# Expert matrix products of a small half tile in four column quarters, and the next slot table formed beside the transposes of the current one

## The chip, the cores and the metric

The kernel runs on one core of a Trainium2 chip. The metric is the device time of one launch in microseconds (us), as the median of three runs. A trace of one further execution shows what each engine did: PE is the matrix engine (PEld its weight loads), DVE the vector engine, ACT the scalar engine, POOL the GpSimd engine, SP the queue that issues the loads.

## What is computed

Two transformer layers over 256 tokens of width 1024. The change touches only the last part, the expert layer of layer 2:

```python
def moe_swiglu(h, router, w_gu, w_d):                 # h: 256 tokens x 1024
    logits = jnp.einsum("bld,de->ble", h, router, preferred_element_type=jnp.float32)
    top_v, top_i = lax.top_k(logits, TOP_K)            # 2 of 8 experts for each token
    top_w = jax.nn.softmax(top_v, axis=-1)
    gates = jnp.sum(jax.nn.one_hot(top_i, N_EXPERTS, dtype=jnp.float32) * top_w[..., None], axis=-2)
    y = gates[..., 0:1] * swiglu(h, w_gu[0], w_d[0])
    for e in range(1, N_EXPERTS):
        y = y + gates[..., e:e + 1] * swiglu(h, w_gu[e], w_d[e])
    return y
def swiglu(h, w_gu, w_d):
    g, u = jnp.split(h @ w_gu, 2, axis=-1)             # 1024 -> 2 x 3584
    return (jax.nn.silu(g) * u) @ w_d                  # 3584 -> 1024
```

All data are float32. The router decides at run time how many tokens an expert has. For the inputs of the reference, worked out by running it, experts 0 to 7 have 68, 69, 55, 38, 145, 46, 29 and 62 tokens.

## The kernel before

**Loads.** The expert weights come from HBM in loads of 128 x 2048 float32 (1024 KB) through a ring of seven buffers (`raw...`, `mraw`); class `Stream` issues a load (line 79) as soon as PE has used up the buffer that it goes into.

**Steps.** Each expert is seven steps; a step is four loads for the gate and up products (`products`, one load each) and two for the down product (`down`). The 56 steps are sorted so that about three experts interleave: in the middle they run as trios such as (4,3), (5,1), (3,6), expert and step. Iteration n of the main loop does the products of step n, with the transposes of step n-1 (`turned`) after the second load, then the gate function of step n (`gated`), then `down` of step n-1.

**Modes.** `modes` chooses at run time by branches. An expert with over 64 tokens has a *full* tile of 128 token slots: its weights are split on ACT and DVE into a high and a low part (lines 102 and 106) and each load is 12 matmuls of 128 columns in the fast float32r format (L1188 to L1190, down L1243 to L1245). Up to 64 remaining tokens make a *half* tile, multiplied in plain float32 without a split (L1196, down L1251): each load is four matmuls with a stationary operand of 64 columns, and the trace shows each as two MATMUL records. Gate and up products go to output partitions 0 to 63 and 64 to 127 of one PSUM tile `PO`, so two matmuls sit side by side in PE's columns. Experts 0 and 1 are full, 2, 3, 5, 6 and 7 half, and 4 is both (128 + 17 tokens).

**Items.** Other work is put into numbered turns, three to a step (3n and 3n+1 ahead of `down`, 3n+2 behind it), at most one item to a turn. For each next expert e there are seven: `prep_p(e)` forms the slot table `P` on DVE (one-hot of token against slot, L1031 and L1033), four `prep_x` gather the tokens by matmuls with `P` (L1041), `prep_g` scales `P` by the gates on POOL (L1054), and `prep_t` transposes it on PE (L1061). `P` has one buffer. Four `scatter` items add an expert's result back (L1109, L1120).

The order on each engine is that of the code: an engine waits in front of an instruction and everything behind it waits as well.

Of the kernel before, what the change touches and what calls it, by code (L numbers as in the profile page):

```python
# [136 lines left out]
def backbone_kernel(ctx, tc, xT, small, const, moe_const, gmw, gmb, modk, modd, wa, wg2, wg4, wo, fgu, fd, mgu, mdn, fing, out):  # L137
# [769 lines left out]
    rank = mo.tile([128, 2, 8], F32, name="rank")  # L907
    rank_h = mo.tile([128, 2, 8], F32, name="rank_h")
    cnt = mo.tile([128, 25], I32, name="cnt")
    none = mo.tile([128, 8], BF16, name="none")  # L910
# [106 lines left out]
    def place(turn, fs):  # L1017

        for f in fs:
            while turn in items:  # L1020
                turn += 1
            items[turn] = f
            turn += 1

    TOGETHER = NS - 3

    def prep_p(e, bank=None):

        P = mp.tile([128, 2, NX], F32, name="P")
        for i in range(2):  # L1030
            nc.vector.tensor_scalar(P[:, i, 0:128], slots, rank[:, i, e:e + 1], None, op0=OP.is_equal)  # L1031
            side = P[:, i, 128:256].rearrange("p (a b) -> p a b", a=2)
            nc.vector.tensor_scalar(side, slots[:, None, 0:64].to_broadcast([128, 2, 64]), rank_h[:, i, e:e + 1], None, op0=OP.is_equal)  # L1033
        X[e] = dict(P=P, x=mp.tile([128, KD, NX], F32R, name="Xe", bufs=LANES), xo=mp.tile([128, KD, 64], F32, name="Xo", bufs=LANES))

    def prep_x(e, d, bank):

        P = X[e]["P"]
        for n in range(2):
            for i in range(2):  # L1040
                mm(bank[:, n * NX:n * NX + SLOTS], tm[:, i, (d + n) * 128:(d + n + 1) * 128], P[:, i, 0:SLOTS], start=i == 0, stop=i == 1)  # L1041
        xe, xo = X[e]["x"][:, d:d + 2], X[e]["xo"][:, d:d + 2]
        v = bank.rearrange("p (n c) -> p n c", n=2)

        def split():
            nc.scalar.copy(xe[:, :, 0:128], v[:, :, 0:128])
            nc.scalar.copy(xo, v[:, :, 128:SLOTS])
            nc.vector.tensor_tensor(xe[:, :, 128:256], v[:, :, 0:128], xe[:, :, 0:128].bitcast(F32), op=OP.subtract)
        post.append(split)
# [6 lines left out]
    def prep_t(e, bank):  # L1056

        P = X[e]["P"]
        for s in range(2):
            for i in range(2):  # L1060
                nc.tensor.transpose(bank[:, s * NX + i * 128:s * NX + (i + 1) * 128], P[:, i, s * 128:(s + 1) * 128], ident)  # L1061
        X[e]["T"] = pt = mp.tile([128, 2, NX], F32, name="Pt", bufs=LANES + 1)
        post.append(lambda: nc.scalar.copy(pt.rearrange("p a b -> p (a b)"), bank))

    def row_halves(a):
# [58 lines left out]

    def modes(e, full, half, bank=None):

        with tc.If(full_[e] > 0) as c:
            full()
            with tc.If(half_[e] > 0) as c2:
                half()  # L1130
            if bank is not None:
                with c2.Else():
                    idle(bank)
        with c.Else():
            half()

    def moe_scr(nm):
        return mp.tile([128, 512], F32, name=nm)

    prep_p(0)  # L1140
    half, most = tiny(), tiny()
    nc.vector.tensor_scalar(half, count, 128.0, None, op0=OP.is_gt)
    nc.vector.tensor_copy(cnt[:, 0:8], count)
    nc.vector.tensor_tensor(half, half, full, op=OP.subtract)
    nc.vector.tensor_copy(cnt[:, 8:16], full)
    nc.vector.tensor_scalar(half, half, 1.0, None, op0=OP.add)
    nc.vector.tensor_reduce(most[:, 0:1], count, axis=mybir.AxisListType.X, op=OP.max)
    nc.vector.tensor_copy(cnt[:, 16:24], half)
# [28 lines left out]
    def products(e, j, po):  # L1177
# [14 lines left out]
        def go_o():  # L1192
            for k in range(2):
                kk = 2 * j + k
                for g in range(2):
                    mm(po[64 * g:64 * g + 64], xo[:, kk, :], w[:, k, g, :], start=kk == 0, stop=kk == KD - 1)  # L1196
        modes(e, go, go_o, po)

    def gated(e, po):
# [3 lines left out]
        def one(t, g, u):  # L1203
            nc.scalar.activation(t, g, AF.Tanh, scale=0.5)
            nc.vector.scalar_tensor_tensor(t, t, 1.0, g, op0=OP.add, op1=OP.mult)  # L1205
            nc.vector.tensor_tensor(t, t, u, op=OP.mult)
        modes(e, lambda: one(tg, PG, PU), lambda: one(to[0:64], po[0:64], po[64:128]))
        return tg, to

    def turned(e, t, po):  # L1210
# [6 lines left out]
        def turn_o():  # L1217
            for k in range(4):
                nc.tensor.transpose(po[:, k * 64:(k + 1) * 64], to[0:64, k * 128:(k + 1) * 128], ident[0:64, 0:64])  # L1219
        modes(e, turn, turn_o, po)  # L1220
        hh, hl = [mp.tile([128, 512], F32R, name=nm) for nm in ("hh", "hl")]
# [8 lines left out]
    def down(e, s, h3):  # L1230
# [4 lines left out]
        for j in range(2):  # L1235
# [11 lines left out]
            def go_o():  # L1247
                for f in range(2):
                    ff = 2 * j + f
                    for b in range(2):  # L1250
                        mm(PYO[64 * b:64 * b + 64], ho[:, ff, :], w[:, f, b, :], start=first and ff == 0, stop=last and ff == 3)  # L1251
            modes(e, go, go_o, PYO)
            st.free()
# [5 lines left out]
    def prep(e):  # L1259
        return [lambda bank: prep_p(e)] + [lambda bank, k=k: prep_x(e, k, bank) for k in range(0, KD, 2)]  # L1260

# [3 lines left out]
    place(0, [prep_back(0)[0]])  # L1265
    place(3, [prep_back(0)[1]])
    for e in range(1, NE):
        begin = 3 * steps.index((e, 0)) - 8
        if e >= LANES:
            begin = max(begin, 3 * steps.index((e - LANES, NS - 1)) + 3)  # L1270
        place(max(begin, 4), prep(e) + prep_back(e))
    for n in range(NE * NS):
        d, ds = steps[n]
        if ds == (NS if d < NE - 1 else TOGETHER) - 1:
            place(3 * n + 5, scatters(d))
    most_ = load_count(24, 4)
    routed.append(True)
# [219 lines left out]
```

## Time and profile before

| | us |
|---|---|
| median of three runs (2123.09 to 2124.11) | 2123.51 |
| the profiled execution, its own time | 2131.55 |
| its span, first to last instruction | 2129.8 |
| expert layer in that span, about | 1085 to 2110 |

Over the span PE is busy 1982.3 us (93%), DVE 1262.7 us (59%), ACT 694.9 us (33%), POOL 445.5 us (21%), and 504.96 MB move at 237 GB/s on average. A busy share says little for a kernel of several stages: what counts is which engine or queue the others wait for in each stretch, and the rows below are picked by stretch.

### The profile page before, as it was taken

The numbers are of one execution on the slowest core, as the hardware profiler recorded it, in microseconds if no ns is written. First come the engines' busy times: TensorE is split into PE (matmuls) and PEld (weight loads), VectorE is DVE, ScalarE is ACT, GpSimd is POOL, SyncE is SP. The second block draws the span as 40 slices with busy tenths as digits, with TensorE's granted clock in tenths as the row PEclk, the third lists the DMA queues.
The fourth block names the chain that finished last, engine by engine and source line by source line (L and its number), as shares of the span: only waits on it lengthen the run. The fifth ranks groups of instructions, "written<-read, shape, count | busy, mean of one in ns | idle before, by whom it ended". The sixth has DMA issues, their size and how long they took to land. (4 is left out here: it accounts for less than half of the span.)

```text
span 2129.8 us, 30212 instructions
## 1 busy us (share of the span) xinstructions
PE 1982.3 (93%) x9396; PEld 1336.3 (63%) x9396; DVE 1262.7 (59%) x1877; ACT 694.9 (33%) x903; POOL 445.5 (21%) x187
## 2 busy tenths in 40 slices
PE   7999889989999988999999999998999999999886
PEld 5776668878888767889977765545444444443222
DVE  7488788759968753765568866454444444432122
ACT  4334332332222223454446645232223222210000
POOL 4433234234443335525310000000000000000000
PEclk8999999999999999999989999999999999999998
DMA  6323234334444544234648899899897888879995
GB/s 260 115 75 111 70 114 168 133 119 157 154 153 171 200 172 172 94 102 153 215 174 295 303 336 372 310 387 361 306 350 284 319 322 320 346 306 415 418 418 231
DMA packets 79319, 504.96 MB, mean 237 GB/s; under 512 B 8785, under 2 KB 9425, under 8 KB 28881
## 3 DMA queue, kind: packets, MB, share of 16 engines
q1 hardware_dynamic: 79056, 501.64, 62.4%
q8 instruction: 143, 2.34, 0.4%
q14 instruction: 120, 0.97, 0.1%
HBM read 500.55 MB, written 1.05 MB: 236 GB/s over the span
## 5 line engine op out<-in xcount | busy, mean ns | idle before, releaser
L1196 PE MATMUL PO<-raw,Xo 128*64 128x512 f32 x1152 | 270.6, 602 | 11.5 <-DMA raw<-in_mgu_dram 11.4
L106 POOL TENSOR_TENSOR w0l<-raw,w0h 128x2048 fp32r<-128x2048 f32 (+6 forms) x43 | 156.8, 3647 | 254.1 <-ACT w0h L102 234.5
L106 POOL TENSOR_TENSOR w1l<-raw,w1h 128x2048 fp32r<-128x2048 f32 (+6 forms) x42 | 153.4, 3652 | 215.4 <-ACT w1h L102 201.4
L1054 POOL TENSOR_SCALAR P<-P,gates 128x256 f32<-128x256 f32 x16 | 21.1, 1326 | 807.1 <-PE PT L1041 517.8
L226 DVE CUSTOM_DVE_ANT_0 scr<-mraw,crows,mcol 128x512 f32<-128x512 f32 x128 | 173.9, 1359 | 4.6
L1196 PEld LDWEIGHTS PO<-raw,Xo 128*64 128x64 f32 x1152 | 77.4, 137 | 157.1 <-issue 155.2
L226 DVE CUSTOM_DVE_ANT_0 scr<-mraw,crows 128x512 f32<-128x512 f32 x128 | 154.9, 1210 | 32.3 <-DMA mraw<-in_modd_dram 32.2
L102 ACT CAST w1h<-raw 128x2048 fp32r<-128x2048 f32 (+3 forms) x82 | 142.2, 1734 | 41.9 <-PE mm L447 22.6
L102 ACT CAST w0h<-raw 128x2048 fp32r<-128x2048 f32 (+3 forms) x82 | 141.1, 1721 | 42.6 <-PE mm L447 29.0
L446 PE MATMUL mm<-Hh,w0h 128*128 128x512 f32 (+1 forms) x380 | 142.3, 384 | 10.9 <-ACT Hh L384 4.2
L1251 PE MATMUL PYO<-raw,ho 128*64 128x512 f32 x584 | 139.5, 608 | 7.0 <-DMA raw<-in_mdn_dram 6.3
L447 PE MATMUL mm<-Hl,w0h 128*128 128x512 f32 (+1 forms) x380 | 141.2, 381 | 5.2 <-POOL Hl L440 5.2
L1205 DVE SCALAR_TENSOR_TENSOR to<-to,PO 64x512 f32<-64x512 f32 x42 | 28.5, 678 | 189.2 <-ACTq L98 122.9
L446 PE MATMUL mm<-Hh,w1h 128*128 128x512 f32 (+1 forms) x384 | 134.8, 362 | 1.9 <-DVE scr L791 1.9
L447 PE MATMUL mm<-Hl,w1h 128*128 128x512 f32 (+1 forms) x384 | 133.9, 360 | 0.0
L106 DVE TENSOR_TENSOR w1l<-raw,w1h 128x2048 fp32r<-128x2048 f32 (+3 forms) x49 | 103.5, 2112 | 37.2 <-ACT w1h L102 36.9
L1227 ACT COPY ho<-PO 128x256 f32<-128x256 f32 x42 | 15.7, 374 | 290.4 <-PE PO L1219 290.4
L106 DVE TENSOR_TENSOR w0l<-raw,w0h 128x2048 fp32r<-128x2048 f32 (+3 forms) x48 | 97.8, 2037 | 9.8 <-ACT w0h L102 9.5
L106 DVE TENSOR_TENSOR w2l<-raw,w2h 128x2048 fp32r<-128x2048 f32 (+3 forms) x45 | 90.9, 2021 | 20.0 <-ACT w2h L102 12.6
L1251 PEld LDWEIGHTS PYO<-raw,ho 128*64 128x64 f32 x584 | 39.9, 139 | 92.9 <-issue 91.2
L449 PE MATMUL mm<-Hh,w0l 128*128 128x512 f32 (+1 forms) x380 | 95.2, 373 | 2.1 <-POOL w0l L106 2.1
L102 ACT CAST w2h<-raw 128x2048 fp32r<-128x2048 f32 (+2 forms) x45 | 81.5, 1812 | 32.3 <-PE PU L1189 23.9
(449 smaller groups left out, 4176.6 us busy)
## 6 DMA issues: line engine op xcount, KB each, us to landing
raw<-in_mgu_dram SPq DMA_DIRECT2D x191, 1024.0 KB, 7.5
raw<-in_mdn_dram SPq DMA_DIRECT2D x97, 1024.0 KB, 8.1
mraw<-in_modd_dram SPq DMA_DIRECT2D x80, 512.0 KB, 4.7
mraw<-in_mgu_dram SPq DMA_DIRECT2D x33, 1024.0 KB, 8.4
raw<-in_fgu_dram SPq DMA_DIRECT2D x22, 1024.0 KB, 4.8
raw<-in_wg_dram SPq DMA_DIRECT2D x28, 640.0 KB, 3.9
raw<-in_wa_dram SPq DMA_DIRECT2D x15, 1024.0 KB, 4.9
mraw<-in_mdn_dram SPq DMA_DIRECT2D x15, 1024.0 KB, 7.3
```

Of the source, the lines that this page charges most:

```text
L102: self.nc.scalar.copy(c.hi[:, :n], c.raw[:, :n])
L106: eng.tensor_tensor(c.lo[:, a:b], c.raw[:, a:b], c.hi[:, a:b].bitcast(F32), op=OP.subtract)
L226: nc.vector.tensor_tensor_reduce(scr(), w[:, h * 512:(h + 1) * 512], crows[:, v, h * 512:(h + 1) * 512], scale=1.0, scalar=mcol[:, l, v, i ...
L446: mm(p[:, :n], wh(k), ah(k), start=first and k == ks[0], stop=False)
L447: mm(p[:, :n], wh(k), al(k), start=False, stop=False)
L449: mm(p[:, :n], wl(k), ah(k), start=False, stop=last and k == ks[-1])
L1054: nc.gpsimd.tensor_scalar(P[:, i, :], P[:, i, :], gates[:, i, e:e + 1], None, op0=OP.mult)
L1196: mm(po[64 * g:64 * g + 64], xo[:, kk, :], w[:, k, g, :], start=kk == 0, stop=kk == KD - 1)
L1205: nc.vector.scalar_tensor_tensor(t, t, 1.0, g, op0=OP.add, op1=OP.mult)
L1227: modes(e, split, lambda: nc.scalar.copy(ho, po[:, 0:256]))
L1251: mm(PYO[64 * b:64 * b + 64], ho[:, ff, :], w[:, f, b, :], start=first and ff == 0, stop=last and ff == 3)
```

## The change

1. A tile of up to 32 tokens (after 128 are taken off for a full expert) becomes a *quarter* tile. `half_[e]` is now 1 for a quarter and 2 for a half, and `modes` asks once more. By the token counts, experts 4 (17 left) and 6 (29) run as quarters, 42 loads each.
2. In a quarter the two products over successive 128 rows of the contraction, which were added up in one PSUM range, go to separate ranges of 32 partitions. A load is still four matmuls, now of 32 columns, at columns 0, 64, 32 and 96. The gate function adds the two parts (`one_q`: six DVE operations where there were two); for the down product the scatter adds them, because the slot table holds such tokens twice (`side`, `upper`, `wide`).
3. `prep_p(e + 1)` is no item of its own any more: it runs on DVE behind `prep_t(e)`, and has one more operation. So the items behind it move one turn forward.
4. Ahead of the first table stand three more small DVE operations, and two more ahead of the counts; POOL clears the tile `to` once.

```diff
-    def prep_p(e, bank=None):
+    def prep_p(e):
         P = mp.tile([128, 2, NX], F32, name="P")
+        side = mp.tile([128, 128], F32, name="side")
+        nc.vector.scalar_tensor_tensor(side.rearrange("p (a b) -> p a b", b=64), upper[:, None, :].to_broadcast([128, 2, 64]), wide[:, e:e + 1],
+                                       slots[:, None, 0:64].to_broadcast([128, 2, 64]), op0=OP.mult, op1=OP.add)
         for i in range(2):
             nc.vector.tensor_scalar(P[:, i, 0:128], slots, rank[:, i, e:e + 1], None, op0=OP.is_equal)
-            side = P[:, i, 128:256].rearrange("p (a b) -> p a b", a=2)
-            nc.vector.tensor_scalar(side, slots[:, None, 0:64].to_broadcast([128, 2, 64]), rank_h[:, i, e:e + 1], None, op0=OP.is_equal)
+            nc.vector.tensor_scalar(P[:, i, 128:256], side, rank_h[:, i, e:e + 1], None, op0=OP.is_equal)
...
         post.append(lambda: nc.scalar.copy(pt.rearrange("p a b -> p (a b)"), bank))
+        if e + 1 < NE:
+            post.append(lambda: prep_p(e + 1))
...
+        def side():
+            if quarter is None:
+                half()
+            else:
+                with tc.If(half_[e] > 1) as c3:
+                    half()
+                with c3.Else():
+                    quarter()
...
+    nc.vector.scalar_tensor_tensor(most, full, -128.0, count, op0=OP.mult, op1=OP.add)
+    nc.vector.tensor_scalar(wide, most, 32.0, -1.0, op0=OP.is_le, op1=OP.mult)
+    nc.vector.tensor_scalar(upper, slots[:, 0:64], 32.0, 32.0, op0=OP.is_ge, op1=OP.mult)
     prep_p(0)
...
+        def go_q():
+            for k in range(2):
+                for g in range(2):
+                    a = 64 * g + 32 * k
+                    mm(po[a:a + 32], xo[:, 2 * j + k, 0:32], w[:, k, g, :], start=j == 0, stop=j == 3, tile_position=(0, a))
...
+        def one_q():
+            s, t = moe_scr("gq")[0:32], to[0:32]
+
+            def both(r):
+                nc.vector.tensor_copy(s, po[r:r + 32])
+                nc.vector.tensor_tensor(s, s, po[r + 32:r + 64], op=OP.add)
+            both(0)
+            nc.scalar.activation(t, s, AF.Tanh, scale=0.5)
+            nc.vector.scalar_tensor_tensor(t, t, 1.0, s, op0=OP.add, op1=OP.mult)
+            both(64)
+            nc.vector.tensor_tensor(t, t, s, op=OP.mult)
...
+            def go_q():
+                for f in range(2):
+                    for b in range(2):
+                        a = 64 * b + 32 * f
+                        mm(PYO[a:a + 32], ho[:, 2 * j + f, 0:32], w[:, f, b, :], start=first and j == 0, stop=last and j == 1, tile_position=(0, a))
...
-        return [lambda bank: prep_p(e)] + [lambda bank, k=k: prep_x(e, k, bank) for k in range(0, KD, 2)]
+        return [lambda bank, k=k: prep_x(e, k, bank) for k in range(0, KD, 2)]
```

On PE, the first load of the products before: twelve matmuls of a full tile (the last is the first row here), then the half tile behind a branch, or the placeholder of an expert without one, or the half tile alone.

```order
L1190 MATMUL PU<-w0l,Xe 128x512
L1129 COMPARE_AND_BRANCH
L1196 MATMUL PO_8524<-raw_7969,Xo 64x512 x4
L1129 UNCONDITIONAL_BRANCH
L1123 LDWEIGHTS none
L1123 MATMUL PO_8524<-none 8x8
L1129 UNCONDITIONAL_BRANCH
L1196 MATMUL PO_8524<-raw_7969,Xo 64x512 x4
```

The same place on PE now (the line numbers have moved: L1196 is L1221, and L1227 is the quarter).

```order
L1215 MATMUL PU<-w0l,Xe 128x512
L1147 COMPARE_AND_BRANCH
L1140 COMPARE_AND_BRANCH
L1221 MATMUL PO_8526<-raw_7969,Xo 64x512 x4
L1140 UNCONDITIONAL_BRANCH
L1227 MATMUL PO_8526<-raw_7969,Xo 32x512 x4
L1140 UNCONDITIONAL_BRANCH
L1132 LDWEIGHTS none
L1132 MATMUL PO_8526<-none 8x8
L1147 UNCONDITIONAL_BRANCH
L1140 COMPARE_AND_BRANCH
L1221 MATMUL PO_8526<-raw_7969,Xo 64x512 x4
```

Each half tile now stands behind one more branch, and beside it four matmuls with 32 output partitions.

On DVE, the table of expert 4 before: it stands behind the gate function of step (2,4) (`to`) and the weight split of a later load (`w2l`), directly ahead of the gather that PE then does with it.

```order
L1205 SCALAR_TENSOR_TENSOR to<-to,PO_8524 64x512
L1206 TENSOR_TENSOR to<-to,PO_8524 64x512
L1127 UNCONDITIONAL_BRANCH
L98 COMPARE_AND_BRANCH
L106 TENSOR_TENSOR w2l<-raw_13150,w2h 128x2048
L98 UNCONDITIONAL_BRANCH x2
L1031 TENSOR_SCALAR P<-mst,rank 128x128
L1033 TENSOR_SCALAR P<-mst,rank_h 128x128
L1031 TENSOR_SCALAR P<-mst,rank 128x128
L1033 TENSOR_SCALAR P<-mst,rank_h 128x128
L1048 TENSOR_TENSOR Xe<-PT,Xe 128x2x128
```

The table of expert 4 on DVE now: behind the drains of iteration 14 (`YO`, `Y`), six steps ahead of its gather.

```order
L1089 TENSOR_TENSOR YO<-PYO,YO 128x512
L1084 UNCONDITIONAL_BRANCH x2
L1084 COMPARE_AND_BRANCH
L1089 TENSOR_TENSOR Y<-PY,Y 128x512 x2
L1084 UNCONDITIONAL_BRANCH x2
L1034 SCALAR_TENSOR_TENSOR side<-upper,wide,mst 128x128
L1037 TENSOR_SCALAR P<-mst,rank 128x128
L1038 TENSOR_SCALAR P<-side,rank_h 128x128
L1037 TENSOR_SCALAR P<-mst,rank 128x128
L1038 TENSOR_SCALAR P<-side,rank_h 128x128
```

What stood ahead of the table in DVE's order, a gate function and a weight split of the same iteration, stands behind it now.

## Rows read from the trace of the kernel before

**Rows 1.** Busy time by stretch (us), PE's granted clock, DMA share, GB/s.

```profile
core 0: us, PE busy (x) PEld busy (x) DVE busy (x) ACT busy (x) POOL busy (x), PEclk, DMA share, GB/s
1384.00:1490.00 106.00, 96.19 (x421) 51.48 (x421) 49.42 (x48) 32.97 (x35) 0.94 (x2) 0.97 0.95 374
1490.00:1900.00 410.00, 392.45 (x1718) 185.76 (x1714) 175.87 (x178) 108.42 (x120) 6.70 (x5) 0.98 0.82 318
1975.00:2100.00 125.00, 104.40 (x439) 32.29 (x440) 25.18 (x37) 7.71 (x16) 0.00 (x0) 0.99 1.01 418
```

**Rows 2.** Waits of PE from 1100 to 2130: total us, times, longest.

```profile
PE PT L1041 <- DVE P L1033: 23.6, 5, 6.2
```

**Rows 3.** The same view of 1960 to 2110 alone: PE's longest wait for loads.

```profile
PE PO L1196 <- DMA raw<-in_mgu_dram: 11.4, 17, 1.5
```

**Rows 4.** Timeline of ACT, 1690 to 1746: start us, duration us; gate functions alone.

```profile
1691.83 0.59 ACT L1204 ACTIVATE to<-PO 64x512 f32<-64x512 f32 x1 [1.96 <-PE PO L1196]
...
1703.68 0.58 ACT L1204 ACTIVATE to<-PO 64x512 f32<-64x512 f32 x1
...
1721.20 0.59 ACT L1204 ACTIVATE to<-PO 64x512 f32<-64x512 f32 x1 [3.13 <-PE PO L1196]
...
1745.40 0.59 ACT L1204 ACTIVATE to<-PO 64x512 f32<-64x512 f32 x1 [1.96 <-PE PO L1196]
```

**Rows 5.** Groups of the whole span: count, busy us, mean ns; loads.

```profile
L1196 PE MATMUL PO<-raw,Xo 128*64 128x512 f32 x1152 | 270.6, 602 | 11.5 <-DMA raw<-in_mgu_dram 11.4
raw<-in_mgu_dram SPq DMA_DIRECT2D x191, 1024.0 KB, 7.5
```

**Rows 6.** Timeline of PE within a step of expert 4, full and half in turn.

```profile
1738.28 0.40 PE L1190 MATMUL PU<-w0l,Xe 128*128 128x512 f32 x1
1738.60 1.94 PE L1196 MATMUL PO<-raw,Xo 128*64 128x512 f32 x8
1740.47 0.50 PE L1188 MATMUL PG<-w2h,Xe 128*128 128x512 f32 x1
```

**Rows 7.** Timeline at 1910, within half tiles: one pair of PE's weight loads.

```profile
1910.41 0.14 PEld L1196 LDWEIGHTS PO<-raw,Xo 128*64 128x64 f32 x2 [0.29 <-issue]
```

**Rows 8.** Timeline around the gather of expert 4, all engines.

```profile
1462.79 2.29 DVE L106 TENSOR_TENSOR w0l<-raw,w0h 128x2048 fp32r<-128x2048 f32 x1 [0.20 <-ACT w0h L102]
1465.00 0.67 DVE L1205 SCALAR_TENSOR_TENSOR to<-to,PO 64x512 f32<-64x512 f32 x1
...
1466.55 0.29 DVE L1031 TENSOR_SCALAR P<-mst,rank 128x128 f32<-128x128 f32 x1
...
1467.08 2.93 PE L1041 MATMUL PT<-P,tm 128*128 128x192 f32 x8 [6.18 <-DVE P L1033]
...
1477.30 1.57 PE L1041 MATMUL PT<-P,tm 128*128 128x192 f32 x8
```

**Rows 9.** By stretch, as rows 1: six us behind each of the five waits.

```profile
1347.87:1353.87 6.00, 6.00 (x17) 5.33 (x18) 0.76 (x3) 0.54 (x2) 0.00 (x0) 0.54 0.25 107
1467.08:1473.08 6.00, 6.00 (x16) 5.29 (x17) 0.77 (x3) 0.54 (x2) 0.00 (x0) 0.51 0.61 250
1604.43:1610.43 6.00, 6.00 (x18) 3.47 (x20) 0.77 (x3) 1.63 (x3) 0.00 (x0) 0.58 0.41 172
1748.12:1754.12 6.00, 6.00 (x22) 2.70 (x24) 0.76 (x3) 0.54 (x2) 0.00 (x0) 0.72 0.25 105
1882.33:1888.33 6.00, 6.00 (x20) 5.09 (x20) 0.77 (x3) 0.54 (x2) 0.00 (x0) 0.70 0.43 179
```

**Rows 10.** Timeline at the first table: PE's wait, and a small DVE operation.

```profile
1079.31 0.56 PE L1041 MATMUL PU<-P,tm 128*128 128x192 f32 x2 [1.73 <-DVE P L1033]
1079.82 0.16 DVE L1142 TENSOR_SCALAR tiny<-tiny 128x8 f32<-128x8 f32 x1
```

**Rows 11.** Waits of ACT and DVE for a branch, 1100 to 2130; the half tile's gate operation.

```profile
ACT w1h L102 <- ACTq L1129: 4.7, 11, 0.7
L1206 DVE TENSOR_TENSOR to<-to,PO 64x512 f32<-64x512 f32 x42 | 29.0, 690 | 1.5
```

## What the change will do to the time

> **What bounds the kernel now.** I read the expert layer by stretches, because its parts have different limits. In the view by stretch, PE is busy 392 of the 410 us from 1490 to 1900 while loads move at 318 GB/s; from 1975 to 2100 it is the other way round, PE 104 of 125 us and 418 GB/s [rows 1]. So up to about 1900 PE sets the pace, and from then on the loads do. The waits agree: PE waits for the products' weight loads 17 times between 1960 and 2110, and the same view from 1100 on has no more than these 17 [rows 3]. From here "the DMA tail" is what comes after about 1900.
>
> Next, how long a step lasts. ACT's gate functions mark the ends of the products. Through one trio, (5,1), (3,6), (4,4), they start at 1691.83, 1703.68, 1721.20 and 1745.40: 11.9, 17.5 and 24.2 us, together 53.6 us for 18 loads [rows 4]. A load is 1024 KB, 1.049 MB [rows 5], so the trio takes 352 GB/s where the tail shows that 418 are to be had.
>
> Third, the waits of PE. One line stands out: five waits for the slot table, 23.6 us in all, the longest 6.2 [rows 2]. The timeline of that one shows why: PE is ready for the gather at 1460.90 (1467.08 less 6.18), but DVE has to finish a weight split and a gate function first and starts the table at 1466.55 [rows 8]. The table itself is short (0.29 us for an operation) and its inputs have been there since the router. It is late only because of where it stands in DVE's order.
>
> **The quarters.** In a half tile one pair of weight loads comes every 0.14 + 0.29 = 0.43 us [rows 7]; that is one pass of two column halves side by side. The records say the same: 1152 of them with a mean of 602 ns would be 693 us, but the group is busy 270.6 us, 0.235 us for each and so 1.88 for the eight of a load [rows 5]. A load is four such passes, 1.72 us, and where full and half tiles alternate the next full matmul starts 1.87 us behind the first half one [rows 6]; the 0.15 between is the switch.
>
> No row shows four column quarters. From below, four run side by side as the two do, and a load is two passes, 0.86 us. From above, they don't overlap at all: four matmuls of two passes each, 8 x 0.43 = 3.44 us. I take 0.86, since two halves of one matmul each already overlap fully in these rows. So a quarter load saves 0.86 us of PE.
>
> The Trainium skill ("TensorE: Matmul & The Clock Gate", Measured speedup vs the span model) has three column tiles of 32 at 2.38 times one, not 3 times. At that efficiency, 0.79, four would be 3.17 times and a load 3.44 / 3.17 = 1.08 us, an estimate from that page; the sum below would be 12 us smaller. The halves here show no such loss, and no row shows quarters.
>
> How many loads count? Expert 4 has 7 steps of 6 loads, 42, all in the stretch that PE sets: 42 x 0.86 = 36.1 us. Expert 6 has 42 too, but only those of (6,0) and (6,1) come ahead of the tail: 12 x 0.86 = 10.3 us. The other 30 gain nothing, as PE only waits longer for the same bytes.
>
> Can the loads follow? A trio with 6 quarter loads falls to 53.6 - 5.2 = 48.4 us, or 390 GB/s, under the 418. Two trios hold expert 6 as well: 43.3 us, where 18 loads at 418 GB/s take 45.2. That is 1.9 us short, twice; the ring of seven buffers and the other items in these trios should cover it, so I count the 10.3 in full.
>
> **The table.** It now stands behind the transposes of the expert before, steps ahead of its gather, so the five waits go: 23.6 us. They cost more than themselves, because PE's granted clock is low behind each. In the six us behind the five it is 0.54, 0.51, 0.58, 0.72 and 0.70, with PE busy throughout [rows 9]: the engine had sat idle and came back at 1.2 GHz for part of the time. Lost there are 6 x (0.46 + 0.49 + 0.42 + 0.28 + 0.30) = 11.7 us; one sees it in the gather itself, eight matmuls in 2.93 us against 1.57 [rows 8]. Together 35.3 us. What is late next? Behind the gather of expert 4 come two loads of a full down product. The split of the second ends at 1465.08 [rows 8]; PE would be past two gathers (2 x 1.57) at 1464.0 and has a whole full load ahead of that one, so nothing waits. On DVE the table now waits for PE's transposes, and behind it are queued the next splits and gate functions; those need buffers that PE frees only later.
>
> **What it costs.** Ahead of the first gather PE already waits 1.73 us for DVE; three small operations at 0.16 [rows 10] and one more of the table's size at 0.29 [rows 8] make 0.8 us. The quarter's gate function has four more operations at 0.69 [rows 11], 2.8 us in each of 14 steps. They are hidden: the transposes come only behind the down product and two more loads, and DVE is busy 176 of 410 us [rows 1]. Without that cover it would be 39 us. One more branch stands ahead of each half tile, on PE, DVE and ACT: nothing where an engine runs ahead, and at most what ACT waits for one now, 4.7 us in 11 times [rows 11], 0.43 for each of expert 4's 14 full down loads, 6 us; between them I take 2.5. Expert 6 now alternates quarters and halves, some four switches in each of two steps at 0.15 [rows 6]: 1 us. POOL's clearing of `to` is hidden, as nobody needs the tile before the first half tile.
>
> **The sum.** 36.1 + 10.3 + 35.3 - 0.8 - 2.5 - 1.0 = 77.4 us. From the profiled execution's 2131.55 us that leaves 2054.2. The median of the runs without profile is 8 us lower, 2123.5, and the same saving gives 2046.
>
> **Rivals.**
> *Weight loads show.* With half as many passes the loads of the stationary operand may no longer hide: 0.14 us [rows 7] in both passes adds 0.27 us to each of the 54 loads, 14.6 us, 2061. For it: twice as many weight loads per pass. Against it: they have 0.29 us of room now. The page named above gives a similar loss. Chance 0.10.
>
> *Loads become the bound early.* Between 1384 and 1490 loads move at 374 GB/s with a DMA share of 0.95 [rows 1]. If mixed steps get no more than that, a trio takes 50.5 us, 2.1 more than wanted, seven times, and expert 6's 10.3 are gone: 25 us, 2071. Against it: 418 in the tail. Chance 0.12.
>
> *The table's wait is replaced by another*, such as one for a split or for the transposes behind POOL's scaling. Then the quarters alone remain: 46.4 - 4.3 = 42 us, 2081. Against it: the splits in rows 8 are done in time. Chance 0.08.
>
> *Quarters run two at a time.* Then a load takes what it takes now and only the table counts, 35.3 - 4.3 = 31 us, 2092. For it: four streams from SBUF at once is something no row shows. Chance 0.05.
>
> *Quarters run one after another*, the case on the other side. A load then takes 3.44 us, 1.72 more: 54 x 1.72 = 93 us, and in the tail 3.44 against the 2.51 that a load takes at 418 GB/s, 30 x 0.93 = 28 us more, so 93 + 28 - 31 = 90 us slower, 2213. It turns from gain to loss where a quarter load takes 1.72 + 31/54 = 2.3 us. Chance 0.03.
>
> **How the numbers follow.** The forecast has 0.60, the rivals 0.38, and 0.02 are for what I don't see. The low end is the sum without costs and with the loads of (6,2) as well (6 x 0.86 = 5.2): 86.9 us less, 2037. The high end takes in the first three rivals, 2082; what is left out is 0.10 of the cases and the edges of the others. Faster by over 0.2% (about what a measurement of this kernel can tell from no change) holds in all but the last rival: 0.95, the same 0.01, slower 0.04.
>
> **What would show it.** In the new trace: four weight loads to each pass of a quarter, and a load of 32-column matmuls in 0.86 us; the trio's three gate functions 48 us apart; no wait of PE for the table beyond the first; a granted clock near 1 behind the gathers; a tail that starts earlier but is as long, still at 418 GB/s. I would be wrong if quarter loads take 1.7 us or more, if the gathers of experts 3 to 7 wait for something else for as long, or if loads hold PE up before the tail.

## The result and the profile after

The changed kernel takes 2095.47 us (median of four runs, 2085.46 to 2099.12), the kernel before 2123.81 us beside it: a ratio of 0.9854 (95% interval 0.9816 to 0.9891), 28 us faster. The forecast was 2046 us, range 2037 to 2082. So the direction was right and the size was not: 28 of 77 us. The profiled execution took 2096.31 us.

First what came as expected. PE's timeline within a step of expert 4 (start us, duration us), with the quarter's weight loads, answers to [rows 6, 7]; ACT's gate functions of the trio (4,3), (5,1), (3,6), (4,4) answer to [rows 4], and the gathers to [rows 8]:

```profile
1699.21 0.16 PEld L1227 LDWEIGHTS PO<-raw,Xo 128*32 128x32 f32 x8 [0.35 <-issue]
1699.21 1.06 PE L1227 MATMUL PO<-raw,Xo 128*32 128x512 f32 x8
1700.20 0.50 PE L1213 MATMUL PG<-w1h,Xe 128*128 128x512 f32 x1
...
1664.54 0.63 ACT L1246 ACTIVATE to<-gq 32x512 f32<-32x512 f32 x1 [2.92 <-DVE gq L1244]
1676.21 0.59 ACT L1235 ACTIVATE to<-PO 64x512 f32<-64x512 f32 x1 [1.05 <-PE PO L1221]
1691.91 0.59 ACT L1235 ACTIVATE to<-PO 64x512 f32<-64x512 f32 x1 [3.37 <-PE PO L1221]
1714.47 0.63 ACT L1246 ACTIVATE to<-gq 32x512 f32<-32x512 f32 x1 [2.92 <-DVE gq L1244]
...
1461.03 1.57 PE L1048 MATMUL PO<-P,tm 128*128 128x192 f32 x8 [0.23 <-issue]
1469.82 1.57 PE L1048 MATMUL PT<-P,tm 128*128 128x192 f32 x8
```

The next full matmul starts 0.99 us behind the first quarter one, where it was 1.87 [rows 6]: four quarters run side by side, and a load saves 0.88 us. The trio takes 49.9 us instead of 53.6, where the forecast had 48.4. The gathers no longer wait for the table, and the first two take 1.57 us each, so the clock is up behind them too.

Now the view of waits, PE from 1100 to 2095 (total us, times, longest us). It answers to [rows 2, 3]:

```profile
PE PO L1227 <- issue: 18.6, 9, 3.3
PE PO L1221 <- issue: 14.3, 16, 2.4
PE PT L1118 <- DVEq L1095: 7.4, 2, 4.4
...
PE PYO L1294 <- issue: 6.9, 10, 1.3
...
PE PT L1115 <- DVEq L98: 2.4, 1, 2.4
```

No wait for the slot table `P` is left, nor one for a load. In their place stands "issue", some 40 us ahead of half and quarter matmuls: time in which PE waits for nothing that the profile shows. The view of before has no such line. By stretch (columns as in [rows 1]):

```profile
1490.00:1860.00 370.00, 346.48 (x1710) 165.36 (x1708) 194.48 (x214) 103.98 (x118) 5.52 (x5) 0.98 0.92 350
1940.00:2065.00 125.00, 95.48 (x423) 27.62 (x423) 31.96 (x47) 7.32 (x16) 0.00 (x0) 0.86 0.98 395
```

In the middle PE is idle 6% of the time, where it was 4%, and in the tail the loads move at 395 GB/s instead of 418, so something holds them up. One such stop in PE's timeline:

```profile
1898.17 0.46 PE L1262 MATMUL PO<-idn,to 64*128 64x64 f32 x4
1901.90 3.19 PE L1227 MATMUL PO<-raw,Xo 128*32 128x512 f32 x16 [3.28 <-issue]
1905.03 1.94 PE L1294 MATMUL PYO<-raw,ho 128*64 128x512 f32 x8
1907.66 1.94 PE L1294 MATMUL PYO<-raw,ho 128*64 128x512 f32 x8 [0.70 <-issue]
```

PE stands still for 3.28 us, and the two quarter loads behind it take 3.19 us instead of some 1.9, at a granted clock of 0.58 (1901.9 to 1905.0). What PE's sequencer did meanwhile is in the view by source line: the branch `with tc.If(full_[e] > 0)` of `modes`, before (L1127) and after (L1145), as count, then min/median/max ns:

```profile
L1127 PEldq COMPARE_BRANCH  x504: 65/208/1328, 1085.9 to 2105.8; - x168
```

```profile
L1145 PEldq COMPARE_BRANCH  x504: 65/208/4267, 1087.7 to 2071.5; - x168
```

The same branch, as often, at the same median, but the longest took 4.27 us instead of 1.33. The page's part on DMA queues has the other half of it. The queue that fetches PE's instructions, before and after (packets, MB, share of 16 engines):

```profile
q8 instruction: 143, 2.34, 0.4%
```

```profile
q8 instruction: 193, 3.16, 0.6%
```

So 50 more packets of 16 KB of instructions. The raw records of the trace, put side by side for the stretch above, join the two (the first is the stop just shown):

```
us        packets of 16 KB on the queue    long branches of PE's sequencer
1898.33                                    3.41 us, to 1901.74
1899.32   1.06 us, to 1900.38
1904.84                                    2.53 us, to 1907.37
1904.91   1.10 us, to 1906.01
1909.91                                    3.21 us, to 1913.12
1910.56   1.09 us, to 1911.65
```

Each long branch ends about 1.4 us after a fetch has landed. From 1100 us on 54 branches of PE take over 0.6 us, and all 54 end 1.3 to 1.7 us after the end of a fetch, where 5% of the shorter ones do; 39 take over 2 us. Before there were 5 and 1. In every version one of these, of 3.5 to 4.4 us, stands behind the expert layer. ACT's and DVE's branches stay under 0.1 us in both.

### The profile page after: what moved, and what is told of

Same layout as the page of the kernel before. It is cut to its first block, busy times and chain, and to the rows that moved or that the text cites. A ratio compares the mean times of both kernels' runs of the same rounds, so it can differ in the third digit from the quotient of the medians.

```text
span 2094.2 us, 31796 instructions
## 1 busy us (share of the span) xinstructions
PE 1922.0 (92%) x9396; PEld 1304.7 (62%) x9396; DVE 1300.0 (62%) x1946; ACT 695.6 (33%) x903; POOL 445.9 (21%) x188
## 5 line engine op out<-in xcount | busy, mean ns | idle before, releaser
L1221 PE MATMUL PO<-raw,Xo 128*64 128x512 f32 x768 | 186.3, 620 | 11.3 <-issue 10.0
L226 DVE CUSTOM_DVE_ANT_0 scr<-mraw,crows 128x512 f32<-128x512 f32 x128 | 165.3, 1292 | 40.7 <-DMA mraw<-in_modd_dram 40.6
L226 DVE CUSTOM_DVE_ANT_0 scr<-mraw,crows,mcol 128x512 f32<-128x512 f32 x128 | 161.1, 1259 | 4.6
L1221 PEld LDWEIGHTS PO<-raw,Xo 128*64 128x64 f32 x768 | 55.3, 142 | 115.7 <-issue 114.3
L1294 PE MATMUL PYO<-raw,ho 128*64 128x512 f32 x392 | 95.5, 620 | 11.4 <-issue 5.6
L106 DVE TENSOR_TENSOR w0l<-raw,w0h 128x2048 fp32r<-128x2048 f32 (+3 forms) x48 | 97.8, 2037 | 9.7 <-ACT w0h L102 9.0
L1236 DVE SCALAR_TENSOR_TENSOR to<-to,PO 64x512 f32<-64x512 f32 x28 | 18.9, 676 | 126.0 <-ACTq L98 78.8
L446 PEld LDWEIGHTS mm<-Hh,w0h 128*128 128x128 f32 x380 | 73.1, 192 | 25.2 <-ACT Hh L384 4.8
```

Of the source, the lines that this page charges most:

```text
L106: eng.tensor_tensor(c.lo[:, a:b], c.raw[:, a:b], c.hi[:, a:b].bitcast(F32), op=OP.subtract)
L226: nc.vector.tensor_tensor_reduce(scr(), w[:, h * 512:(h + 1) * 512], crows[:, v, h * 512:(h + 1) * 512], scale=1.0, scalar=mcol[:, l, v, i ...
L446: mm(p[:, :n], wh(k), ah(k), start=first and k == ks[0], stop=False)
```

## Experiments

Theory 1: the code that the change adds to each load makes PE wait for instructions, and this took what the quarters gave. Rivals: the loads became the bound early; the longer gate function of the quarter costs the time (theory 2); the tail gives back what was saved ahead of it (theory 3). All runs in one table. The ratio is to the kernel before as it ran beside each of them (medians 2121.60 to 2124.41 us); the columns on the right are from the profiled executions: the first and last gate function of the expert layer, and from 1100 us on the fetches of PE's instructions and PE's branches over 2 us:

| | median us | ratio to before (95%) | first, last gate | fetches, long branches |
|---|---|---|---|---|
| before | 2123.81 | | 1098.8, 2100.0 | 101, 1 |
| the change | 2095.47 | 0.9854 (0.9816 to 0.9891) | 1100.6, 2064.9 | 151, 39 |
| table_only | 2095.64 | 0.9862 (0.9846 to 0.9878) | 1098.6, 2066.3 | 101, 1 |
| never_quarter | 2119.75 | 0.9983 (0.9969 to 0.9996) | 1099.6, 2085.4 | 151, 29 |
| static_choice | 2062.72 | 0.9722 (0.9705 to 0.9738) | 1090.2, 2031.1 | 100, 2 |
| code_once | 2226.90 | 1.0481 (1.0463 to 1.0498) | 1105.3, 2194.4 | 105, 2 |
| once_idle | 2095.23 | 0.9861 (0.9830 to 0.9893) | 1103.6, 2066.5 | 108, 1 |
| never_x2 | 2207.22 | 1.0389 (1.0359 to 1.0420) | 1095.2, 2177.7 | 192, 78 |
| static_defer | 2061.52 | 0.9710 (0.9682 to 0.9739) | 1091.3, 2024.8 | 101, 1 |
| static_act | 2065.76 | 0.9713 (0.9681 to 0.9745) | 1098.7, 2035.3 | 101, 1 |
| behind_full | 2075.28 | 0.9778 (0.9760 to 0.9796) | 1099.5, 2042.7 | 126, 9 |
| static_e4 | 2067.41 | 0.9740 (0.9722 to 0.9759) | 1099.1, 2038.8 | 101, 1 |
| behind_full_defer | 2067.11 | 0.9738 (0.9720 to 0.9755) | 1101.1, 2038.0 | 127, 12 |
| x2_half_loads | 2093.24 | 0.9850 (0.9812 to 0.9888) | 1092.6, 2061.5 | 191, 21 |

The first gate function varies from 1090 to 1105 us although all versions have about the same work ahead of it. That blurs a median by a few us, so differences are also read from gate to gate; that is one execution of each version, and before's was 8 us above its median.

**table_only**: the table's move without the quarters.

```diff
-    nc.vector.tensor_scalar(wide, most, 32.0, -1.0, op0=OP.is_le, op1=OP.mult)
+    nc.vector.tensor_scalar(wide, most, -4096.0, -1.0, op0=OP.is_le, op1=OP.mult)
-        modes(e, go, go_o, go_q, po)
+        modes(e, go, go_o, None, po)
...
-            modes(e, go, go_o, go_q, PYO)
+            modes(e, go, go_o, None, PYO)
```

> The quarter code is left out and no tile counts as a quarter; the move of the slot table stays. It measures the table's part by itself. My forecast had 35.3 us less 0.8 us at the front, about 34 us, so 2090; the new trace of the change reads about 32 us, 2092. Theory 1 (the longer code of each load is what ate the quarters' gain: PE's sequencer waits for instructions at the branches): 2088 to 2095, with no long idle time of PE before L1221 put down to issue. Rival 2 (the loads become the bound early, so that neither part can give its due): also about 2092, as the full trios need fewer bytes per us than the quarter trios. Rival 3 (the table's wait was only replaced by others): 2110 to 2124.

Measured: 28 us faster than before, from gate to gate 967.7 us instead of 1001.2. It takes as long as the whole change: the quarters, as they were written, brought nothing. The tail is at full rate and clock, which clears the table's move of what was seen there:

```profile
1940.00:2065.00 125.00, 102.72 (x438) 31.39 (x436) 25.17 (x37) 7.71 (x16) 0.00 (x0) 1.00 1.01 418
```

**never_quarter**: the program of the change, with the first edit above alone.

> The program of the change, word for word on every engine, but the threshold for a quarter is one that no tile meets, so that the quarter code stands in the program and never runs. Against the kernel with the table move alone it adds code, one branch for each half tile, and nothing else. Theory 1 (waiting for instructions): 30 to 45 us slower than that kernel, 2120 to 2137, with idle time of PE put down to issue in front of L1221 and the down line. Rival 2 (loads bound early): no load is shorter here, so within 5 us of the table kernel. Rival 3 (the longer gate function of the quarter costs the time): as rival 2, since that function never runs.

Measured: 24 us slower than table_only (18 from gate to gate), by code that never runs and the branch ahead of it. Its waits of PE, as the change's above; the instruction queue moves the same 193 packets:

```profile
PE PO L1221 <- issue: 16.8, 13, 2.2
PE PYO L1294 <- issue: 13.3, 9, 2.2
```

Neither early loads nor a longer gate function can do this; only theory 1 had foreseen it, and too large (30 to 45). That the branch costs it, and not the code behind it, is left to never_x2.

**static_choice**: `modes` takes the quarter or the half when the program is written.

```diff
-            if quarter is None:
-                half()
-            else:
-                with tc.If(half_[e] > 1) as c3:
-                    half()
-                with c3.Else():
-                    quarter()
+            if quarter is not None and e in (4, 6):
+                quarter()
+            else:
+                half()
```

> Which experts are quarters is decided when the program is written (4 and 6, right for these inputs alone): their half code is replaced by the quarter code, the others have the half code alone. So a load has as much code as before the change, with both gains in. Theory 1 (waiting for instructions): the quarters' 46 us come out in full beside the table, 2045 to 2055, and the idle time put down to issue is gone. Rival 2 (loads bound early): about as the change, 2085 to 2099. Rival 3 (the longer gate function): as the change too, 2085 to 2099, since that function runs here just as often.

Measured: 33 us faster than the change (23 from gate to gate), 61 faster than before; fetches and long branches are as before the change. So the code for choosing cost the change 23 to 33 us. But the quarters' 46 us are not all there: 33 us against table_only, 27 from gate to gate.

**code_once** writes the choice once.

```diff
-        with tc.If(full_[e] > 0) as c:
+        with tc.If(full_[e] > 0):
             full()
-            with tc.If(half_[e] > 0) as c2:
-                side()
-            if bank is not None:
-                with c2.Else():
-                    idle(bank)
-        with c.Else():
+        with tc.If(half_[e] > 0) as c2:
             side()
+        if bank is not None:
+            with c2.Else():
+                idle(bank)
```

> The choice between half and quarter is written once for each load, behind the full tile, where the change has it twice (behind the full tile, and for experts without one). The products, gate functions and results are the same, and it works for any inputs. Theory 1 (waiting for instructions): a load then has about as much code on PE as before the change, so most of the lost time comes back: 2050 to 2070. Rivals 2 and 3: no change against the kernel with the change, 2085 to 2099.

Measured: 103 us slower than before. That was a miss of the edit, not of the theory. First PE's timeline, then the view of the source line that holds the branch (count, then min/median/max ns):

```profile
1500.95 1.94 PE L1219 MATMUL PO<-raw,Xo 128*64 128x512 f32 x8 [0.45 <-PEq L1145]
1503.34 1.94 PE L1219 MATMUL PO<-raw,Xo 128*64 128x512 f32 x8 [0.45 <-PEq L1145]
```

```profile
L1145 PEldq EVENT_SEMAPHORE  x245: 51/51/51, 1253.3 to 2204.2; - x123
```

Where the full tile is skipped, its arm has no work on PE, and the sequencer stands at a semaphore instruction until PE's own matmuls are done. It does so 245 times; PE's waits for it add up to 132 us in 219 times. The fetches are down to 105, with 2 long branches.

**once_idle** mends that with the placeholder.

```diff
+        if spare is not None:
+            with tc.If(full_[e] > 0) as c:
+                full()
+            with c.Else():
+                idle(spare)
+            with tc.If(half_[e] > 0) as c2:
+                side()
+            with c2.Else():
+                idle(bank)
+            return
```

> As the kernel with the choice written once, but where the full tile is skipped PE runs one placeholder matmul into a PSUM bank that is free, as the change has it for a skipped half tile. In the kernel without it PE stood still 0.45 us ahead of nearly every half load, with its sequencer at the branch behind the full tile: it waited for its own last matmul to end. Theory 1 (instruction fetch is what ate the gain; the still stands are an artefact of a branch arm without work for PE): with the still stands gone, code about as long as before the change gives about what the static choice gives, 2060 to 2072. Rival (the two branches for each load cost PE by themselves): 2095 or more.

Measured: 2095.23, as the change and not as the static choice. The fetches are down to 108 with one long branch, so that part came true, but the placeholder has a price of its own, as PE's timeline shows:

```profile
1563.31 0.17 PE L1132 MATMUL PY<-none 128*8 128x8 bf16 x1
1563.41 1.94 PE L1304 MATMUL PYO<-raw,ho 128*64 128x512 f32 x8
1565.28 0.17 PE L1132 MATMUL PG<-none 128*8 128x8 bf16 x1
```

A half load now comes every 1.97 us instead of 1.87. For the 210 loads of the five experts without a full tile that is at most 21 us (in the tail PE has time to spare). The kernel takes 22 us longer than the static choice from gate to gate, and 33 by the medians, so up to 12 us are not traced. The rival's number, 2095 or more, came true as well: a price of the two branches by themselves isn't ruled out here.

**never_x2**: never_quarter with the unused matmuls written twice.

```diff
                 with c3.Else():
                     quarter()
+                    if bank is not None:
+                        quarter()
```

> The kernel whose quarters never run, with the quarter's matmuls of products and down written twice, so that about 32 more instructions for each load stand in the program and never run; no branch is added. Theory 1 (waiting for instructions): the cost of unused code grows with its length, at least as much again, 24 us, and more in the tail where short loads follow each other: 2145 to 2200. Rival (what costs is the added branch, not the length): 2116 to 2124, as with the code once.

Measured: 2207.22, 87 us more than never_quarter, a bit over the expected range, with no branch added. The length is what costs, and steeply.

**static_defer** and **static_act** were to find the rest of the quarters' gain in the longer gate function on DVE. The first puts `both(64)` and the product of `one_q` behind `run_post()` of the iteration's two items; the second lets ACT copy the whole tile.

```diff
-            both(64)
-            nc.vector.tensor_tensor(t, t, s, op=OP.mult)
+            def rest():
+                both(64)
+                nc.vector.tensor_tensor(t, t, s, op=OP.mult)
+            late[:] = [rest]
...
         item(3 * n + 1, PT)
         run_post()
+        while late:
+            late.pop()()
```

> The static choice, with the second half of the quarter's gate function (three DVE operations, 2.1 us) put behind the additions of the scatter's first banks; the same operations, in another order on DVE. In the trace of the static choice PE waits 2.37, 4.69 and 3.60 us for a bank that DVE has not read yet, because the quarter's gate function stands ahead of that on DVE. Theory 2 (the longer gate function took the rest of what the quarters should have given): the three waits shrink by about 2 us each and the low clock behind them with it, 6 to 12 us faster than the static choice, 2051 to 2057. Rival (the rest was lost to the loads): 2060 to 2066.

```diff
-            both(0)
+            nc.scalar.copy(q, po)
+            nc.vector.tensor_tensor(s, s, po[32:64], op=OP.add)
             nc.scalar.activation(t, s, AF.Tanh, scale=0.5)
             nc.vector.scalar_tensor_tensor(t, t, 1.0, s, op0=OP.add, op1=OP.mult)
-            both(64)
+            nc.vector.tensor_tensor(s, q[64:96], po[96:128], op=OP.add)
             nc.vector.tensor_tensor(t, t, s, op=OP.mult)
```

> The static choice, with the quarter's two copies out of PSUM taken from DVE: ACT copies the whole tile once (512 columns, about 0.6 us), and DVE has four operations where it had six. Theory 2 (the longer gate function on DVE): DVE is done 1.4 us earlier, less 0.6 for ACT's copy ahead, so the three waits shrink by about 1 us each, 3 to 6 us faster than the static choice, 2057 to 2060. Rival (the rest was lost to the loads): 2060 to 2066.

Measured: 2061.52 and 2065.76, by the medians no gain that can be told from the static choice's 2062.72: both lie in the rival's range. From gate to gate the first is 7.4 us shorter and the second 4.3, as theory 2 had it, but one profile each does not settle that. A pair below, behind_full and behind_full_defer, tries it again.

**behind_full** keeps the choice behind a full tile alone; it has half of the added code, and works for any inputs.

```diff
         with c.Else():
-            side()
+            half()
...
     nc.vector.tensor_scalar(wide, most, 32.0, -1.0, op0=OP.is_le, op1=OP.mult)
+    nc.vector.tensor_tensor(wide, wide, full, op=OP.mult)
```

> The change with the quarter code only behind a full tile; a tile that stands alone is always a half (so expert 6 is one again), and it works for any inputs. A load's code on PE is then 16 instructions longer than before the change, where the change has 32. Theory 1 (waiting for instructions, at a price that rises steeply with the length: nothing for 0, about 24 us for 32 instructions, 87 more for the next 32): 16 cost 12 us at most, probably about 5; against the kernel with the table move alone expert 4's quarters bring some 25 to 32, so 2066 to 2080. Rival (the cost goes with the added choice itself, not with the length): 7 of 8 experts still have it ahead of none of their tiles but behind a full one, so this says little; with the length priced evenly, 12 us, 2078 to 2083.

**static_e4** is static_choice with `e == 4` for `e in (4, 6)`, and 20 tokens as the bound.

> The static choice with expert 4 alone as quarters; expert 6 is a half tile again. It measures what expert 6's quarters bring where code length plays no part. My forecast had 10.3 us for them, so 2073. Theory 3 (what they save ahead of the tail is given back in it, as the tail is a matter of bytes: from its step 44 on the static kernels take about 5 us longer than the kernel with the table move alone, with PE's granted clock at 0.83 to 0.91 there instead of 1.00): 2062 to 2068.

Measured: 2075.28 and 2067.41. Both have expert 4 alone as quarters, so the 16 instructions and the choice cost 8 us by the medians, 3.5 from gate to gate; the steep price fits, and the even one of 12 lies at the edge of what these intervals leave. That the price is steep is shown by never_x2. Against static_choice, expert 6's quarters are worth 4.7 us by the medians (the intervals overlap) and nothing from gate to gate (940.9 and 939.7), not 10.3: theory 3 holds as to size. The stretch of 125 us that begins 45 us behind the tail's start in static_choice (at 1860, from when on loads move at 417 GB/s) has a granted clock of 0.86:

```profile
1905.00:2030.00 125.00, 98.71 (x446) 27.86 (x443) 33.34 (x49) 7.82 (x16) 0.00 (x0) 0.86 1.01 413
```

The loads go at 413 GB/s, near the 418 of the tail before: there a shorter load of PE gives nothing, and PE, idle more often, comes back at a lower clock (0.86, where table_only had 1.00).

**behind_full_defer** adds the edit of static_defer, with `rest` under `tc.If(half_[e] > 0)` and `tc.If(half_[e] < 2)`.

> As the kernel with the quarter code only behind a full tile, with the second half of the quarter's gate function put behind the additions of the scatter's first banks. Theory 2 (the longer gate function holds up the scatter's banks): 4 to 8 us faster than without. Rival (nothing to be had there; in the runs of the static choice the medians differed by 1 us, though the expert layer of the profiled run was 7 us shorter): within 3 us of it.

Measured: 2067.11, 8.2 us faster than behind_full, and the intervals (0.9720 to 0.9755, 0.9760 to 0.9796) do not touch; from gate to gate it is 6.3 us. So the gate function's place costs time, as theory 2 had it. The same place in DVE's and PE's order, first without the edit, then with it:

```profile
1498.30 0.68 DVE L1250 TENSOR_TENSOR to<-to,gq 32x512 f32<-32x512 f32 x1
...
1500.65 0.68 DVE L1129 TENSOR_TENSOR xt<-xt,PT 128x512 f32<-128x512 f32 x1
1501.47 1.10 PE L1115 MATMUL PT<-Y,Pt 128*128 128x512 f32 x2 [2.37 <-DVEq L98]
```

```profile
1500.90 0.68 DVE L1129 TENSOR_TENSOR xt<-xt,PT 128x512 f32<-128x512 f32 x1
1501.61 0.69 DVE L1244 COPY gq<-PO 32x512 f32<-32x512 f32 x1
1501.73 1.10 PE L1115 MATMUL PT<-Y,Pt 128*128 128x512 f32 x2 [0.21 <-DVE xt L1129]
```

PE's second scatter writes the bank `PT` that DVE must have added to `xt` first. With the whole gate function ahead of that addition PE waits 2.37 us, with half of it 0.21. That is 2.2 us of the 8.2. From the first to the last gate function PE is idle 45 us without the edit and 42 with it, so most of the rest is not traced to a wait, and why the same edit gave 1 us by the medians on the static choice stays open. This is also the best version of those that leave the choice to run time: 57 us faster than before and 28 faster than the change.

**x2_half_loads** asks why a fetch comes late. Each expert load moves its first half, and the code uses it twice.

```diff
-            self.nc.sync.dma_start(c.raw[:, :c.cols], c.ap)
+            m = c.cols // 2 if c.when else c.cols
+            self.nc.sync.dma_start(c.raw[:, :m], c.ap[:, :m])
...
-                    mm(po[64 * g:64 * g + 64], xo[:, kk, :], w[:, k, g, :], start=kk == 0, stop=kk == KD - 1)
+                    mm(po[64 * g:64 * g + 64], xo[:, kk, :], w[:, 0, g, :], start=kk == 0, stop=kk == KD - 1)
```

> The kernel with the unused quarter code written twice (2207 us), with half of each expert load left out: 64 KB less for every 128 KB, so 512 KB instead of 1024, and PE, ACT and DVE use the half that is there twice. PE's work and code are the same, the result isn't that of the reference. It asks why an instruction fetch comes late. If the loads keep the DMA busy and the fetch waits among them: the long branches of PE's sequencer nearly vanish (78 over 2 us in the kernel with full loads, then under 15), and the time falls to what PE needs, about 2055 to 2085. If a fetch takes that long by itself: most of the long branches stay, 50 or more, and the time is 2140 or more.

Measured: 2093.24, and 21 branches over 2 us where never_x2 has 78. It lies between the two expectations. The view by stretch from 1080 to 1900 (columns as in [rows 1]), never_x2 first:

```profile
1080.00:1900.00 820.00, 753.88 (x3289) 424.18 (x3289) 424.94 (x388) 293.85 (x276) 18.47 (x14) 0.99 0.84 311
```

```profile
1080.00:1900.00 820.00, 804.31 (x3577) 442.13 (x3575) 444.58 (x415) 302.46 (x294) 21.55 (x16) 1.00 0.51 173
```

With the same code PE is busy 804 us instead of 754 when the DMA engines are half free, about as much as table_only is there with full loads (807). Branches over 0.6 us fall from 107 to 71, but their sum from 287 to 120 us. So the loads' traffic makes most of the waiting, and fetches are late without it too. The 114 us by which the kernel is faster also hold what half the loads give in the tail; no run has half loads without the added code. What share is the queue and what the path behind it (the 1.4 us from landing to the end of the branch) stays open.

## Why the prediction was wrong, step by step

**The quarters' rate: right.** 0.99 us from quarter to full matmul, 0.86 forecast for the load and 0.15 for the switch. The rivals with weight loads that show, two at a time and one after another are out. "Loads become the bound early" is out as well: in static_choice PE waits for no load ahead of 1860 us. The time that "two at a time" gave, 2092, was nearly met, by another cause.

**The table: right in kind, a little large.** The five waits are gone and the clock behind them is up. 28.1 us by the medians, where the sum had 35.3 less 0.8; the 33.5 from gate to gate hold the 8 us by which before's profiled execution lay above its median. The 0.8 was too small: two of the three small operations took 0.79 and 1.19 us, not 0.16, while a POOL addition ran, and PE's first wait for the table is 4.70 us where it was 1.73, so 3.0 more:

```profile
1078.24 1.19 DVE L1161 TENSOR_SCALAR wide<-tiny 128x8 f32<-128x8 f32 x1
...
1081.54 2.56 PE L1048 MATMUL PU<-P,tm 128*128 128x192 f32 x8 [4.70 <-DVE P L1038]
```

**The step that failed: "One more branch stands ahead of each half tile ... 0.43 for each of expert 4's 14 full down loads, 6 us; between them I take 2.5."** I priced the branch itself at 2.5 us, by what ACT waited for one [rows 11], and took 6 us for the upper bound; what came was 23 to 33 us. What the change adds to PE is less a branch than 32 instructions for every load (eight weight loads and eight matmuls in each of two places), most of them never run. With the branch they cost 24 us where no quarter runs (never_quarter against table_only; 18 from gate to gate) and 33 where quarters do (the change against static_choice; 23). That a shorter load leaves a fetch less time may be why, but isn't tried by itself. With 16 it was 8, with 64 it was 112 (never_x2 against table_only). The Trainium skill ("Runtime: NRT & Kernel Launch", Instruction fetch mechanics) says that PE's instructions come in blocks of 16 KiB by a DMA queue of their own, that the next block is fetched beside the current one so that the cost of a new block is mostly hidden, and that a branch to code that isn't there yet waits for a fetch. The trace agrees as to the blocks (16384 bytes in each packet) and the wait; "mostly hidden" fits the kernel before, 5 long branches with 101 fetches, and not the change, 54 with 151. In 27 of the 54 the packet had begun ahead of the branch, so those were not fetches that the branch itself set off. The row that should have warned me, the 143 packets of the instruction queue, stood on the page of before; I had counted only what runs.

**"They are hidden": half wrong.** I named the transposes as the next to need DVE behind the quarter's gate function. What is late first is the addition of the scatter's bank, and PE's next scatter behind it: 2.4 us at the place shown, and 8 us by the medians with expert 4 alone (behind_full against behind_full_defer), most of which no wait shows.

**Expert 6 and the tail: too large.** "I count the 10.3 in full", but static_e4 leaves between 0 and 5 us for them. The tail is not "as long": from the gate function of step (5,5) to the last one table_only takes 164.4 us and static_defer 169.3. From step (7,1), two on, it is 140.5 and 140.6: from there on the loads' bytes set the pace in both, and the ground is lost just ahead of it. That a PE that is early gets there with fewer loads in hand is argued, not tried by itself.

**The sum again.** Forecast: table 34.5, quarters 45.4, the branch -2.5, together 77.4. Measured by the medians: table 28.1 (before to table_only), quarters 32.9 (table_only to static_choice), code -32.8 (static_choice to the change), together 28.2. From gate to gate: 33.5, 26.8 and -23.4, together 36.9. Either way the code took about what the quarters gave, and the quarters gave less than their 45.4.

## What to carry to other kernels

Count the instructions that a branch skips as well as those that run: an alternative written into every load lengthens the code that the engine must fetch, and here, with the DMA engines 84 to 100% busy, PE waited at its branches for it. Look at the instruction queue on the page before adding an arm, put a choice in only where it can pay (behind_full has most of the gain with half of the code), and don't leave an arm without work on an engine whose order the others count. When an operation is made longer off the critical path, follow everything that is queued behind it on its engine to the first one that somebody waits for.

## What the runs showed of the hardware

- Four fp32 matmuls with 32 output columns each, over 128 rows and 512 columns, run fully side by side: two passes of about 0.43 us for eight records (0.86 to 0.88 us from one quarter load to the next at full clock).
- A late instruction fetch held PE's sequencer at a branch for 0.6 to 4.3 us (54 branches of the change, 128 us in all); PE's matmuls stood still for some 44 us with no other cause in the profile. Every one of the 54 ended 1.3 to 1.7 us behind the end of a 16 KB packet, which itself takes about 1.0 us.
- Code that never runs cost 24 us for 32 instructions in each of 336 loads, and 112 us for 64; both hold one more branch for each half tile. With half the load traffic PE was busy 804 of the 820 us up to 1900 us with the 64, against 754 with all of it.
- A branch around PE's matmuls without a second arm that has work on PE made PE drain where it was skipped: 245 times, 132 us of waiting; a placeholder matmul in its place cost 0.10 us.
